# A hybrid decoder layer: the MLP's gate and up as seven block products, its down projection as a separate pass

## Chip, core, metric

One core of a Trainium2 chip runs the whole layer as one program. The metric is device time in microseconds; the kernel before takes 3286.72 us (median of 3 runs, 3285.8 to 3287.6). Engines: PE is TensorE (matrix products), PEld its weight loads, DVE is VectorE, ACT ScalarE, POOL GpSimd, and SP (SyncE) issues every DMA of this kernel.

## What is computed

A decoder layer on 2048 tokens of width 1024: token mixing (attention and a state space), cross-attention, and a gated MLP. Only the MLP changes:

```
hn   = rms_norm(h, norm_ffn)                       # [2048, 1024]
gate, up = split(hn @ w_ffn_up)                    # 2 x [2048, 2816]
gate = causal_dwconv(gate, conv_w, conv_b)         # 3 taps along the tokens
h    = h + (silu(gate) * up) @ w_ffn_down          # [2048, 1024]
```

All values are float32. A product a x b is done in three passes: each operand is split into a high part that TensorE's fp32r format holds exactly and a low remainder, and lo x hi, hi x lo and hi x hi are summed in PSUM (`mm3`, lines 63 to 67). A split is one ScalarE copy and one VectorE subtraction (`split`, lines 70 to 72).

## The kernel before

Everything is feature-major: 128 features on the partitions, tokens along the free axis, 512 tokens per PSUM bank. Order of the stages: input projection with the state space beside it, attention, `StageC` (output projection, cross-attention and its projection, 512 tokens at a time), then `StageD`, the MLP.

`StageC.run` ends with the cross-attention's output projection over four chunks c of 512 tokens. For each of 8 output tiles it does 24 products (8 feature tiles x 3 passes), loads h1 (L1390), adds (L1391) and stores the residual `h2D` (L1392). The operands of odd chunks lie in the pool `ca1`, those of even chunks in `even`, on the right side of SBUF. After chunk 2 the right side is handed on (`ahead`, `Dn.begin`), and the MLP's first loads run beside chunk 3.

`StageD.work` takes the tokens in two halves of 1024. Per half it holds the residual of 8 feature tiles in SBUF (`hacc`, L1413) and its scaled split (`hx`). The norm's factor r by token is applied behind the products. There are NFF = 22 tiles of 128 hidden features, in groups of four. Per tile: load and split the 512 KB weights of gate and up; for each 512 tokens 24 products for gate, the convolution, SiLU (VectorE, ScalarE, one GpSimd product, L1489 to L1499), 24 products for up, and the split of the result. After a group the down projection adds its share to `hacc` in SBUF: 8 output tiles x 2 token blocks, each of 12 products and one VectorE addition (L1511). So a half has 22 x 2 x 2 x 24 = 2112 products of gate and up and 1056 of down; both halves 4224 and 2112.

The code is written as a data flow. At build time a planner allocates the tiles and orders each engine's queue and SP's queue by the order of the text and by when it expects each input and buffer; the chip then runs each queue strictly in that order. A tile of a pool waits for the last reader of the buffer that it takes over.

Of the kernel before, what the change touches and what calls it, by code (L numbers as in the profile page):

```python
# [8 lines left out]
F32 = mybir.dt.float32  # L9
# [33 lines left out]
# columns of the packed [128, n] parameter array  # L43
# [55 lines left out]
def exp_acc(nc, scratch, out, x):  # L99
    """exp(x), x below 80, to float32's accuracy on VectorE (small tiles); scratch gives tiles of x's shape."""  # L100
# [15 lines left out]
class SumSq:  # L116
    """Sum over tiles of their squares, [128, n]."""
# [90 lines left out]
def stage_a(ctx, K, xT, win, wf, memT, wxk, wxv, qD, kD, vD, uD, cD, xkD, xvD, side):  # L208
    """Input projection.  First u^T (tokens step-major), then q^T and k^T (normalised, feature-major), f,
    and v as hi and lo; side(ctx) gives the steps of work that goes beside."""  # L210
# [24 lines left out]
    # the pools of the work beside lie below those of the first loads  # L235
# [4 lines left out]
    # with the tokens on partitions: 0.25 * eps * (mean square + eps) by heads, and -2 / rms  # L240
# [3 lines left out]
    # the forget gates' projection, [token in its tile, head, tile]  # L244
# [22 lines left out]
    # column tiles of 256 in win: q 0,1  k 2,3  v 4,5  u 6,7  # L267
# [39 lines left out]
    def qk_begin(p, j, w, g, dst):  # L307
        """256 columns of q or k of two token tiles, normalised by head."""
# [15 lines left out]
    def qk_end(f, p, j, g, dst):  # L324
        """Feature-major, with the norm's gain."""
# [39 lines left out]
def forget(K, tile_, pss, ft, cD):  # L365
    """Forget gate: cumsum(log_sigmoid(f + bias)), worked as [(head, block), token]."""
# [29 lines left out]
    # log f = min(z, 0) - log1p(e)  # L396
# [11 lines left out]
def s5_setup(ctx, K, uD):  # L408
    """Per-state constants of all groups, [(re, im) x state, group], in steps."""
# [4 lines left out]
    # kernels K_m for m = 7..-7 (zero below 0), [channel in, group, m, channel out]  # L414
# [6 lines left out]
    with tc.tile_pool(name="s5t", bufs=1, side="right", reuse_waits="tile") as sp:  # L421
# [36 lines left out]
        # powers lambda^0..8  # L458
# [20 lines left out]
        # decay over a step of 8, and the unit rotation  # L479
# [37 lines left out]
        # zero-order hold: B times (lambda - 1) / a  # L517
# [29 lines left out]
        # c1 = [c_re; -c_im], c2 = [-c_im; -c_re]  # L547
# [8 lines left out]
        # powers in the order of the steps: 7..0, and 8..1  # L556
# [6 lines left out]
        # D, to go into K_0  # L563
# [5 lines left out]
def s5_tables(K, S, sp, b, n=2):  # L569
    """Of groups nb..nb+n-1: the products' weights and the rotation tables."""  # L570
# [10 lines left out]
    def weights(r, i, mr, mi, name, tag):  # L581
        """r m_r + i m_i over (group, step, channel); r, i by step and group, m by group and channel."""
# [30 lines left out]
def s5_prep(K, S, pools, b, tables, n=2):  # L613
    """The products' weights as hi and lo, with the kernels of a chunk's own steps."""
# [14 lines left out]
    # row (step in i, channel in), column (step out 7 - o, channel out): K_{7 - o - i}  # L629
# [46 lines left out]
    # the state before each chunk  # L676
# [23 lines left out]
def s5(ctx, K, uD, yD):  # L700
    """The whole of it, in steps; ctx is the stack of pools around."""
# [21 lines left out]
class Head:  # L723
    """One head of the forgetting attention, in steps that another phase's steps can go between."""

    def __init__(self, K, h, P, qD, kD, vD, cD, oD, lD):
# [3 lines left out]
        # keys [k_hi; k_lo], cumsum on every partition, values [v_hi, v_lo] per key tile, row sums  # L730
# [6 lines left out]
    def prepare(self, fp=None):  # L737
        """Loads the keys, the values and the first queries."""
# [911 lines left out]
```

## Time and profile before

| | |
|---|---|
| median of 3 runs | 3286.72 us |
| profiled execution, first to last instruction (span) | 3283.0 us |
| around the span (median less span) | 3.7 us |
| MLP: first product to end of the span | 1794.3 to 3283.0 us |
| granted TensorE clock, mean over the span | 0.980 |

The profile is one execution. Its page gives the span and no total of its own, so the run's time is read as the span and the 3.7 us around it. Busy shares are averages over stages; what limits a stage is read from the windows and the waits of that stage. A clock of 1.00 is the higher of TensorE's two levels, 2.4 GHz.

### The profile page before, as it was taken

Reading aid. Unit: us, or ns where it says so; the run is one execution under the profiler, and the core shown is the slowest. Engines: PE = TensorE matmul, PEld = TensorE weight load, DVE = VectorE, ACT = ScalarE, POOL = GpSimd, SP = SyncE. Lnnn points to the kernel's source line nnn. Section 1 sums busy time; section 2 is a strip of 40 time slices with the busy share of each in tenths; the row PEclk is TensorE's granted clock in tenths of the full one; section 3 lists DMA queues with packets and bytes.
Section 4 is the critical chain, followed back from the end, with each engine's and each line's share of the span. In section 5 each row is a group of like instructions: output and inputs, shape, how many; then the busy total and the mean of one; then the engine's idle time right before and its main releaser. Section 6 shows DMA issues by size and latency. Waiting matters only on the chain.

```text
span 3283.0 us, 42856 instructions
## 1 busy us (share of the span) xinstructions
PE 3143.8 (96%) x16060; PEld 2617.5 (80%) x16060; DVE 1962.1 (60%) x3474; ACT 1236.4 (38%) x2256; POOL 522.9 (16%) x596
## 2 busy tenths in 40 slices
PE   7898878999999889999999999999999999999999
PEld 6788878888887667888787878888887788888887
DVE  8768899688878856444543544445445544445444
ACT  5443323488878524444422322212122312212121
POOL 3616664001001420000000100001000100001000
PEclk9898989999999999999999999999999999999999
DMA  6853434654444654212345211111113211111111
GB/s 192 159 181 116 143 112 127 189 150 133 116 147 130 183 164 159 76 54 76 120 138 170 61 45 52 45 45 52 45 47 130 68 52 52 39 52 48 43 45 61
DMA packets 253000, 329.50 MB, mean 100 GB/s; under 512 B 91636, under 2 KB 154356, under 8 KB 251640
## 3 DMA queue, kind: packets, MB, share of 16 engines
q1 hardware_dynamic: 252792, 326.76, 33.5%
q8 instruction: 126, 2.06, 0.3%
q14 instruction: 82, 0.67, 0.1%
HBM read 242.17 MB, written 84.52 MB: 100 GB/s over the span
## 4 chain that ended last, share of the span: by engine, by line
PE 78%; DVE 10%; DMA 5%; issue 2%; ACT 2%; POOL 2%; SPq 0%; DVEq 0%; ACTq 0%; POOLq 0%
PE dmm L66 10%; PE dmm L65 10%; PE dmm L67 10%; PE dps L66 5%; PE dps L65 5%; PE dps L67 5%; PE cmm L65 4%; PE cmm L66 4%; PE cmm L67 4%; PE pt L824 3%; PE po L817 2%; PE sps L790 2%; PE po L818 2%; PE sps L791 2%; DVE whl L72 1%
## 5 line engine op out<-in xcount | busy, mean ns | idle before, releaser
L65 PE MATMUL dmm<-hx,whl 128*128 128x512 f32 x1408 | 555.3, 395 | 2.1 <-ACT hx L77 2.1
L66 PE MATMUL dmm<-hx,whl 128*128 128x512 f32 x1408 | 555.5, 395 | 0.6 <-DVE hx L78 0.6
L67 PE MATMUL dmm<-hx,whl 128*128 128x512 f32 x1408 | 555.3, 395 | 0.0
L71 ACT CAST whl<-wraw 128x1024 fp32r<-128x1024 f32 (+3 forms) x251 | 218.0, 871 | 683.2 <-PE dps L67 402.5
L1499 POOL TENSOR_TENSOR gt<-gt,r 128x512 f32<-128x512 f32 x88 | 115.9, 1317 | 1886.3 <-DVE gt L1498 1282.7
L65 PEld LDWEIGHTS dmm<-hx,whl 128*128 128x128 f32 x1408 | 263.6, 187 | 68.4 <-ACT hx L77 3.0
L66 PEld LDWEIGHTS dmm<-hx,whl 128*128 128x128 f32 x1408 | 263.8, 187 | 66.5 <-DVE hx L78 1.2
L67 PEld LDWEIGHTS dmm<-hx,whl 128*128 128x128 f32 x1408 | 263.9, 187 | 65.0
L65 PE MATMUL cmm<-act,whl 128*128 128x512 f32 x760 | 307.2, 404 | 2.6 <-DVE whl L72 1.3
L66 PE MATMUL cmm<-act,whl 128*128 128x512 f32 x760 | 301.7, 397 | 4.1 <-DVE act L72 4.0
L1511 DVE TENSOR_TENSOR hacc<-dps,hacc 128x512 f32<-128x512 f32 x192 | 132.7, 691 | 281.6 <-PE dps L67 281.5
L67 PE MATMUL cmm<-act,whl 128*128 128x512 f32 x760 | 300.6, 396 | 0.0
L72 DVE TENSOR_TENSOR whl<-wraw,whl 128x1024 fp32r<-128x1024 f32 (+3 forms) x251 | 256.5, 1023 | 41.9 <-ACT whl L71 41.7
L66 PE MATMUL dps<-gl,whl 128*128 128x512 f32 x704 | 277.7, 394 | 0.6 <-DVE gl L72 0.6
L65 PE MATMUL dps<-gh,whl 128*128 128x512 f32 x704 | 277.8, 395 | 0.4 <-ACT gh L71 0.3
L67 PE MATMUL dps<-gh,whl 128*128 128x512 f32 x704 | 277.6, 394 | 0.0
L1489 DVE TENSOR_TENSOR g<-dmm,r 128x512 f32<-128x512 f32 x88 | 60.9, 692 | 240.8 <-PE dmm L67 240.8
L814 DVE TENSOR_TENSOR pl<-pt,ph 128x512 fp32r<-128x512 f32 (+1 forms) x320 | 186.8, 605 | 22.5 <-ACT ph L828 21.0
L824 PE MATMUL pt<-pk,sb 128*128 128x128 f32 x1088 | 173.7, 277 | 4.4 <-DVE pl L814 2.4
L66 PEld LDWEIGHTS cmm<-act,whl 128*128 128x128 f32 x760 | 144.3, 190 | 40.3 <-DVE act L72 6.7
L65 PEld LDWEIGHTS cmm<-act,whl 128*128 128x128 f32 x760 | 144.2, 190 | 38.9 <-issue 2.2
L828 ACT CAST ph<-pt 128x512 fp32r<-128x512 f32 (+1 forms) x320 | 158.8, 521 | 39.0 <-PE pt L824 36.6
(448 smaller groups left out, 6684.7 us busy)
## 6 DMA issues: line engine op xcount, KB each, us to landing
wraw<-wup SPq DMA_DIRECT2D x87, 512.0 KB
wraw<-wdn SPq DMA_DIRECT2D x80, 256.0 KB
qhl<-qD SPq DMA_DIRECT2D x128, 128.0 KB
wraw<-win SPq DMA_DIRECT2D x28, 512.0 KB
x<-xT SPq DMA_DIRECT2D x32, 256.0 KB
xr<-xT SPq DMA_DIRECT2D x32, 256.0 KB
kD<-qy SPq DMA_DIRECT2D x32, 256.0 KB
qD<-qy SPq DMA_DIRECT2D x32, 256.0 KB
```

The lines of the kernel that those rows point to most:

```text
L65: nc.tensor.matmul(out, lhsT=al, rhs=bh, start=first, stop=False)
L66: nc.tensor.matmul(out, lhsT=ah, rhs=bl, start=False, stop=False)
L67: nc.tensor.matmul(out, lhsT=ah, rhs=bh, start=False, stop=last)
L71: nc.scalar.copy(hi, src)
L72: (eng or nc.vector).tensor_tensor(lo, src, hi.bitcast(F32), op=ALU.subtract)
L790: nc.tensor.matmul(out, lhsT=ql[:, o : o + 128], rhs=kc, start=True, stop=False)
L791: nc.tensor.matmul(out, lhsT=qh[:, o : o + 128], rhs=kc, start=False, stop=not diag)
L814: v.tensor_tensor(b, c, a.bitcast(F32), op=ALU.subtract)
L824: nc.tensor.transpose(ps[:, j * 128 : (j + 1) * 128], rows[j][:, kt * 128 : (kt + 1) * 128], K.ident)
L828: nc.scalar.copy(ph[:, s], ps[:, s])
L1499: nc.gpsimd.tensor_tensor(t, t, r[:, s], op=ALU.mult)
L1511: v.tensor_tensor(acc[m][:, s], ps, acc[m][:, s], op=ALU.add)
```

## The change

Gate and up weights of one hidden tile form a 2 x 2 block matrix: rows gate and up, columns the two halves of the 1024 features (four 128-tiles each). The operand is 2 x 2 as well: feature halves by two token blocks of 512. The block product takes seven block multiplications in place of eight, with sums of blocks formed beforehand and afterwards. One block multiplication is 4 feature tiles x 3 passes = 12 products of 128 x 512, so one hidden tile and half has 7 x 12 = 84 products in place of 96. Step u runs over 2 x 22 = 44 of them.

- `StageD.sums` scales the residual with the gain and with r, forms the operand's sums on GpSimd and stores seven operands of four tiles to DRAM (`xsD`). The first half's runs beside chunk 3 of `StageC` (`side`), the second half's from u = 4.
- `StageD.operand` loads them back and splits them: 28 tiles per half, all held in `dx`.
- `fast_weights` forms four sums of weight blocks on GpSimd and splits seven blocks of 128 x 512 per step.
- After the products, sums are formed from PSUM: p6 and p7 add onto p1's bank once ScalarE has copied it (`kept`), p3 onto p5's.
- The activations go to DRAM (`hD`). `StageD.down` is a second pass over four blocks of 512 tokens: 8 output tiles, each 22 x 3 = 66 products into one PSUM bank, one addition of the reloaded residual, one store. Its weights are loaded once per token block, 32 x 1.4 MB.

The other lines of the diff delete comments. Its core:

```diff
+STEPS = ("p1", "p2", "p5", "p6", "p3", "p4", "p7")
+def fast_weights(K, pools, ra, rb, q):
+    wp, sp = pools
+    a11, a12, a21, a22 = ra[:, :q], ra[:, q:], rb[:, :q], rb[:, q:]
+    def s(x, y, op):
+        t = sp.tile([128, q, 128], F32, tag="ws", name="wsum")
+        gp.tensor_tensor(t, x, y, op=op)
+        return t
+    def hl(x):
+        t = wp.tile([128, 2, q, 128], F32R, tag="w", name="wf")
+        split(nc, t[:, 0], t[:, 1], x)
+        return t
+    s1 = s(a21, a22, ALU.add)
+    yield hl(a11)
+    s2 = s(s1, a11, ALU.subtract)
+    yield hl(a12)
+    yield hl(s1)
+    s4 = s(a12, s2, ALU.subtract)
+    yield hl(s2)
+    s3 = s(a11, a21, ALU.subtract)
+    yield hl(s4)
+    yield hl(a22)
+    yield hl(s3)
...
+    def begin(self, wup):
+        self.ap, self.rp, self.xp, self.sp = pool("da", 1), pool("dr", 4), pool("dxs", 6), pool("dws", 3)
+        self.acc = self.ap.tile([128, 512], F32, name="sums")
+        self.raws(0)
+        return self.sums(0)
...
+    def sums(self, half):
+        W = 256
+        for o in range(0, 512, W):
+            cols = slice(o, o + W)
+            new = lambda n: self.xp.tile([128, 2, W], F32, tag="xs", name=n)
+            r = new("xr")
+            nc.sync.dma_start(r, e(self.rD[half])[:, :, cols].broadcast_to([128, 2, W]))
+            for k in range(4):
+                s0, s1 = new("xs0"), new("xs1")
+                for t, i in ((s0, k), (s1, k + 4)):
+                    nc.sync.dma_start(t, e(self.h2D[half][i * 128 : (i + 1) * 128])[:, :, cols])
+                    v.scalar_tensor_tensor(out=t, in0=t, scalar=K.g_ffn[:, i : i + 1], in1=r, op0=ALU.mult, op1=ALU.mult)
+                n, t4 = new("xs2"), new("xs3")
+                gp.tensor_tensor(n[:, 1], s1[:, 1], s0[:, 1], op=ALU.subtract)
+                gp.tensor_tensor(s0[:, 1], s0[:, 1], s0[:, 0], op=ALU.subtract)
+                gp.tensor_tensor(n[:, 0], s1[:, 1], s0[:, 1], op=ALU.subtract)
+                gp.tensor_tensor(t4[:, 0], n[:, 0], s1[:, 0], op=ALU.subtract)
+                for t, ix in ((s0[:, 0], 0), (s0[:, 1], 2), (s1[:, 0], 1), (s1[:, 1], 4), (n[:, 0], 3), (n[:, 1], 6), (t4[:, 0], 5)):
+                    nc.sync.dma_start(self.xsD[half][ix, k][:, cols], t)
+                yield
+    def operand(self, half, dx):
+        for ix in range(7):
+            out = []
+            for k in range(4):
+                t = self.xp.tile([128, 512], F32, tag="xs", name="xb")
+                nc.sync.dma_start(t, self.xsD[half][ix, k])
+                x = dx.tile([128, 2, 512], F32R, tag="x", name="xf")
+                split(nc, x[:, 0], x[:, 1], t)
+                out.append(x)
+            yield out
...
+    def up(self, ctx):
+        dx, wp, gp, cp, tp, kp = pool("dx", 28), pool("dw", 8), pool("dg", 2), pool("dc", 4), pool("dt", 2), pool("dk", 1)
+        psm = pool("dpm", 2, space=PSUM)
...
+        for u in range(2 * NFF):
+            self.raws(u + 1)
...
+            if u == 4:
+                more = self.sums(1)
+            bank = {n: psm.tile([128, 512], F32, tag=n, name="d" + n) for n in "abed"}
...
+            for i, n in enumerate(STEPS):
+                last = u == NFF - 1
+                if i + 1 < 7:
+                    w[STEPS[i + 1]] = next(nw)
+                    if xs is not None:
+                        x[STEPS[i + 1]] = next(xs)
+                else:
+                    nw = later
+                    xs = self.operand(1, dx) if last else None
...
+                b = {"p1": "a", "p2": "b", "p5": "e", "p6": "a", "p3": "e", "p4": "d", "p7": "a"}[n]
+                product(bank[b], w[n], x[n], n in ("p1", "p2", "p5", "p4"))
+                if n == "p1":
+                    v.tensor_copy(g[:, 0:2], carry[:, f])
+                    p1 = kept(bank["a"], "kp1")
+                elif n == "p2":
+                    v.tensor_tensor(g[:, 2:514], bank["b"], p1, op=ALU.add)
+                    gate(0)
+                elif n == "p5":
+                    p5 = kept(bank["e"], "kp5")
+                elif n == "p6":
+                    u2 = kept(bank["a"], "ku2")
+                elif n == "p3":
+                    v.tensor_tensor(g[:, 514:], bank["e"], u2, op=ALU.add)
+                    v.tensor_copy(carry[:, f], g[:, 1024:])
+                    gate(1)
+                elif n == "p7":
+                    u3 = kept(bank["a"], "ku3")
+                    v.tensor_tensor(p5, bank["a"], p5, op=ALU.add)
+                    v.tensor_tensor(u3, u3, bank["d"], op=ALU.subtract)
+                    out(0, u3)          # GpSimd product, store to hD
+                    out(1, p5)
+                next(more, None)
...
+    def down(self, ctx, wdn, outT):
+        hp, wp, rp, op = pool("eh", 29), pool("ew", 2), pool("er", 3), pool("eo", 3)
+        psm = pool("epm", 4, space=PSUM)
+        def weights(i):
+            return load_w(K, wp, wdn[i % KT], [128, NFF, 128], parts=2)
+        def operand(c):
+            for k in range(NFF):
+                t = rp.tile([128, 512], F32, tag="hr", name="hraw")
+                nc.sync.dma_start(t, hD[c][k * 128 : (k + 1) * 128])
+                x = hp.tile([128, 2, 512], F32R, tag="h", name="hf")
+                split(nc, x[:, 0], x[:, 1], t)
+                yield x
+        w = weights(0)
+        nxt = list(operand(0))
+        for c in range(NC):
+            h, nxt = nxt, []
+            more = operand(c + 1) if c + 1 < NC else iter(())
+            for m in range(KT):
+                nw = weights(i + 1) if i + 1 < NC * KT else None
+                ps = psm.tile([128, 512], F32, tag="mm", name="dps")
+                nc.sync.dma_start(res, h2D[c // 2][m * 128 : (m + 1) * 128, c % 2 * 512 : c % 2 * 512 + 512])
+                for k in range(NFF):
+                    mm3(nc, ps, w[0][:, k], w[1][:, k], h[k][:, 0], h[k][:, 1], k == 0, k == NFF - 1)
+                    if m == KT - 1:
+                        nxt.extend([t for t in [next(more, None)] if t is not None])
+                v.tensor_tensor(res, ps, res, op=ALU.add)
+                nc.sync.dma_start(outT[m * 128 : (m + 1) * 128, cols], res)
+                w = nw
```

The function `gate` of the new loop keeps the convolution and SiLU of before (ScalarE identity, two VectorE passes, ScalarE tanh, one VectorE pass) on each of the two token blocks.

## Rows read from the trace of the kernel before

**Rows 1.** page, busy time: us, share of the span, instructions

```profile
PE 3143.8 (96%) x16060; PEld 2617.5 (80%) x16060; DVE 1962.1 (60%) x3474; ACT 1236.4 (38%) x2256; POOL 522.9 (16%) x596
```

**Rows 2.** page, costliest groups: products of gate and up, of down

```profile
L65 PE MATMUL dmm<-hx,whl 128*128 128x512 f32 x1408 | 555.3, 395 | 2.1 <-ACT hx L77 2.1
L65 PE MATMUL dps<-gh,whl 128*128 128x512 f32 x704 | 277.8, 395 | 0.4 <-ACT gh L71 0.3
```

**Rows 3.** windows: us, busy us of PE, PEld, DVE, ACT, POOL, clock, DMA, GB/s

```profile
1748.00:1766.00 18.00, 18.00 (x79) 14.50 (x79) 5.32 (x8) 3.16 (x5) 0.00 (x0) 1.00 0.86 300
1795.00:1815.00 20.00, 19.61 (x77) 15.67 (x78) 17.08 (x28) 15.28 (x23) 0.00 (x0) 0.91 0.51 157
2515.00:2555.00 40.00, 39.10 (x165) 30.34 (x164) 28.35 (x46) 15.77 (x26) 0.59 (x1) 1.00 0.78 266
2600.00:3278.00 678.00, 677.92 (x2906) 542.91 (x2905) 309.51 (x488) 143.90 (x199) 50.47 (x39) 1.00 0.16 48
```

**Rows 4.** timeline of TensorE, firsts and lasts of 87 and 85 products

```profile
1719.76 0.39 PE L66 MATMUL cmm<-act,whl 128*128 128x512 f32 x1
1739.87 0.40 PE L65 MATMUL cmm<-act,whl 128*128 128x512 f32 x1
1772.77 0.39 PE L67 MATMUL cmm<-act,whl 128*128 128x512 f32 x1
1791.81 0.39 PE L67 MATMUL cmm<-act,whl 128*128 128x512 f32 x1
```

**Rows 5.** groups by line and shape, 1800 to 3283 us: busy us, mean ns

```profile
L72 DVE TENSOR_TENSOR whl<-wraw,whl 128x512 fp32r<-128x512 f32 x80 | 55.4, 692 | 0.0
L1494 DVE SCALAR_TENSOR_TENSOR gt<-g,pk,gt 128x512 f32<-128x512 f32 x88 | 65.9, 749 | 23.0 <-ACT gt L1493 23.0
L1489 DVE TENSOR_TENSOR g<-dmm,r 128x512 f32<-128x512 f32 x88 | 60.9, 692 | 240.8 <-PE dmm L67 240.8
L71 ACT CAST gh<-gt 128x512 fp32r<-128x512 f32 x88 | 54.7, 621 | 161.7 <-DVE gt L1501 161.7
L1493 ACT ACTIVATE gt<-g,pk 128x512 f32<-128x512 f32 x88 | 71.7, 814 | 187.8 <-DVE g L1489 183.5 <-DVE carry L1491 4.4
L1497 ACT ACTIVATE th<-gt 128x512 f32<-128x512 f32 x88 | 55.6, 632 | 152.6 <-DVE gt L1495 152.6
L1499 POOL TENSOR_TENSOR gt<-gt,r 128x512 f32<-128x512 f32 x88 | 115.9, 1317 | 1886.3 <-DVE gt L1498 1282.7 <-DVE carry L1491 603.6
```

**Rows 6.** groups by line and shape, the whole span, same columns

```profile
L72 POOL TENSOR_TENSOR gl<-g,gh 128x256 fp32r<-128x256 f32 x32 | 23.6, 736 | 164.9 <-ACT gh L71 155.7 <-DVE pl L814 9.2
L1320 ACT COPY xoy<-xov 128x512 f32<-128x512 f32 x32 | 17.5, 592 | 3.6 <-PE xov L67 3.5
L72 DVE TENSOR_TENSOR whl<-wraw,whl 128x1024 fp32r<-128x1024 f32 x151 | 187.5, 1243 | 41.9 <-ACT whl L71 41.7
```

**Rows 7.** timeline of VectorE and GpSimd, 1207 to 1210 us

```profile
1207.34 1.44 POOL L1109 TENSOR_TENSOR fo<-fo 128x512 f32<-128x512 f32 x1 [5.89 <-DMA fo<-oD]
1207.58 1.75 DVE L72 TENSOR_TENSOR act<-nout,act 128x512 fp32r<-128x512 f32 x1
1208.86 1.61 POOL L1110 TENSOR_TENSOR fo<-fo,li 128x512 f32<-128x512 f32 x1
```

**Rows 8.** timeline of SyncE's DMA issues and of one ScalarE wait for a load

```profile
1749.85 3.02 SPq L1413 DMA_DIRECT2D hacc<-h2D  x5
1771.23 0.32 SPq L1392 DMA_DIRECT2D h2D<-h  x1
1773.24 0.32 SPq L1390 DMA_DIRECT2D h<-h1D  x1
1618.48 0.32 SPq L1195 DMA_DIRECT2D hl<-xoD  x1
1621.33 0.62 ACT L71 CAST act<-hl 128x512 fp32r<-128x512 f32 x1 [1.15 <-DMA hl<-xoD]
```

**Rows 9.** timeline of TensorE where the MLP begins

```profile
1794.31 0.49 PE L65 MATMUL dmm<-hx,whl 128*128 128x512 f32 x1 [2.12 <-ACT hx L77]
```

More of the change, by code (lines that the diff above doesn't have):

```diff
@@ L1380, in run @@
         nxt = hn
+        side = iter(())
         for c in range(NC):
@@ L1396, in run @@
                     end3(*late)
+                next(side, None)
             late = (c, sq.acc)
             if c + 2 == NC:
-                ahead()
+                side = ahead()
         self.ctx.close()
-class StageD:
-    def __init__(self, K, h2D, rD, right):
-        self.K, self.h2D, self.rD, self.right = K, h2D, rD, right
-    def load(self, half):
-        self.ac = [self.bp.tile([128, T // 2], F32, tag=f"ac{k}", name="hacc") for k in range(KT)]
-        for k in range(KT):
-            self.K.nc.sync.dma_start(self.ac[k], self.h2D[half][k * 128 : (k + 1) * 128])
-    def begin(self, wup):
-        self.bp = self.right.enter_context(self.K.tc.tile_pool(name="da", bufs=1, side="right", reuse_waits="tile"))
-        self.load(0)
-        self.acc = self.bp.tile([128, 512], F32, name="sums")
-        self.raw = self.bp.tile([128, KT, 128], F32, tag="r", name="graw")
-        self.K.nc.sync.dma_start(self.raw, wup[0])
+STEPS = ("p1", "p2", "p5", "p6", "p3", "p4", "p7")
@@ new lines, in up @@
+        pool = lambda n, b, **k: ctx.enter_context(tc.tile_pool(name=n, bufs=b, reuse_waits="tile", **k))
+        dx, wp, gp, cp, tp, kp = pool("dx", 28), pool("dw", 8), pool("dg", 2), pool("dc", 4), pool("dt", 2), pool("dk", 1)
+        psm = pool("dpm", 2, space=PSUM)
+        cw = kp.tile([128, 3, NFF], F32, name="cw")
+        cb = kp.tile([128, NFF], F32, name="cb")
+        v.tensor_scalar(out=cw, in0=K.p("convw").rearrange("p (i f) -> p i f", i=3), scalar1=0.5, scalar2=None, op0=ALU.mult)
@@ new lines, in up, with product, kept @@
+        v.tensor_scalar(out=cb, in0=K.p("convb"), scalar1=0.5, scalar2=None, op0=ALU.mult)
+        carry = kp.tile([128, NFF, 2], F32, name="carry")
+        v.memset(carry, 0.0)
+        def product(ps, w, x, first):
+            for k in range(4):
+                for j, (a, b) in enumerate(((1, 0), (0, 1), (0, 0))):
+                    nc.tensor.matmul(ps, lhsT=w[:, a, k], rhs=x[k][:, b], start=first and k + j == 0, stop=k == 3 and j == 2, skip_group_check=not first)
+        def kept(ps, n):
+            t = cp.tile([128, 512], F32, tag="c", name=n)
+            nc.scalar.copy(t, ps)
+            return t
@@ new lines, in up, with gate, out @@
+        wps = (wp, self.sp)
+        x, nx = {}, None
+        nw = fast_weights(K, wps, *self.raw.pop(0), 4)
+        xs = self.operand(0, dx)
+        w = {}
+        w[STEPS[0]] = next(nw)
+        x[STEPS[0]] = next(xs)
+        more = iter(())
+        for u in range(2 * NFF):
+            half, f = divmod(u, NFF)
+            self.raws(u + 1)
+            later = fast_weights(K, wps, *self.raw.pop(u + 1), 4) if u + 1 < 2 * NFF else iter(())
+            if u == 2:
+                st = psm.tile([128, 512], F32, tag="d", name="fst")
+                nc.tensor.matmul(st, lhsT=K.ones, rhs=self.acc, start=True, stop=True)
+                K.ln_exp()
+                rl = rinv(K, tp, st, 512, 1.0 / D, EPS, tag="t")
+                nc.sync.dma_start(self.rD[1][:, 512:], rl[0:1])
+            if u == 4:
+                more = self.sums(1)
+            bank = {n: psm.tile([128, 512], F32, tag=n, name="d" + n) for n in "abed"}
+            g = gp.tile([128, 2 + 1024], F32, tag="g", name="g")
+            hs = []
+            def gate(n):
+                o = 512 * n
+                a = lambda i: g[:, o + i : o + i + 512]
+                t = tp.tile([128, 512], F32, tag="t", name="gt")
+                nc.scalar.activation(t, a(2), AF.Identity, bias=cb[:, f : f + 1], scale=cw[:, 2, f : f + 1])
+                v.scalar_tensor_tensor(out=t, in0=a(1), scalar=cw[:, 1, f : f + 1], in1=t, op0=ALU.mult, op1=ALU.add)
+                v.scalar_tensor_tensor(out=t, in0=a(0), scalar=cw[:, 0, f : f + 1], in1=t, op0=ALU.mult, op1=ALU.add)
+                th = tp.tile([128, 512], F32, tag="th", name="th", bufs=1)
+                nc.scalar.activation(th, t, AF.Tanh)
+                v.scalar_tensor_tensor(out=t, in0=th, scalar=1.0, in1=t, op0=ALU.add, op1=ALU.mult)
+                hs.append(t)
+            def out(n, up):
+                nc.gpsimd.tensor_tensor(hs[n], hs[n], up, op=ALU.mult)
+                nc.sync.dma_start(hD[2 * half + n][f * 128 : (f + 1) * 128], hs[n])
+            for i, n in enumerate(STEPS):
[7 more added lines that the diff above has]
+                    xs = self.operand(1, dx) if last else None
+                    if u + 1 < 2 * NFF:
+                        w[STEPS[0]] = next(nw)
+                        nxt = next(xs) if xs is not None else x[STEPS[0]]
+                b = {"p1": "a", "p2": "b", "p5": "e", "p6": "a", "p3": "e", "p4": "d", "p7": "a"}[n]
[21 more added lines that the diff above has]
+                next(more, None)
+            x[STEPS[0]] = nxt
```

119 lines of the change are left out of this document (36 added, 83 removed).

## The prediction, before the result was known

> **What bounds the kernel now.** I read the page's busy times first: TensorE is busy 96% of the span, VectorE 60%, GpSimd 16% [rows 1]. A mean over stages proves little, so I took the windows next: in the MLP TensorE is busy for 677.92 of 678 us at a granted clock of 1.00, and even where the halves meet for 39.1 of 40 [rows 3]. The MLP waits only at its start, 2.12 us for its first split operand [rows 9]. So from 1794 us on the time is the number of products times their spacing; every other engine and the DMAs lie beside it. The spacing is 678 us / 2906 = 0.2333 us [rows 3]; 4224 products of gate and up and 2112 of down (three lines each of x1408 and of x704) [rows 2] make 6336 x 0.2333 = 1478 us of the 1483 us.
>
> The spacing has a second value. In chunk 3 of the stage before, 84 intervals take 1791.81 - 1772.77 = 19.04 us, 0.2267 each; in chunk 2, 86 take 1739.87 - 1719.76 = 20.11, 0.2338 each [rows 4]. Weights, shapes and clock are the same; only the place of the moving operand differs (pool `ca1` against `even`).
>
> **The change, part by part.**
>
> *Fewer products.* 44 x 84 = 3696 in place of 4224; down keeps 2112. At 0.2333 us the 528 that go are worth 123.2 us.
>
> *Their spacing.* The trace can't show it for the new tiles. Its ends are 0.2267 and 0.2338 [rows 4], so between a gain of 5808 x 0.0066 = 38 us and a loss of 3. I take 0.2267. The new operands are tiles of [128, 2, 512] in the first pool opened on the left (`dx`, then `eh`), as those of `ca1` are behind one of whole 64 KB, while `hx`, `gh` and `gl` lie behind the odd 176 bytes of `carry`. The new code opens the pool of `carry` last. This is a correlation, not a mechanism that I can show. 5808 x 0.2267 = 1316.7, so both terms together are 1478.4 - 1316.7 = -161.7 us.
>
> *The loop's other engines, per step of 84 x 0.2267 = 19.04 us.* VectorE: 7 weight splits x 0.692, two gates of 2 x 0.749 + 0.69, four passes on PSUM x 0.692 [rows 5], and two short copies: 12.3 us. ScalarE: 7 x 0.621 + 2 x (0.814 + 0.632) [rows 5] + 4 PSUM copies x 0.592 [rows 6] = 9.6. GpSimd: 4 weight sums and 2 output products x 1.317 [rows 5] = 7.9. DMA: 1 MB in and 0.5 MB out, 80 GB/s, where 300 were moved in a window [rows 3]. None reaches 19. The new waits of TensorE are on PSUM copies, with one product block of 2.7 us (p3 on p5's copy) or two (p6, p7) between, for a copy of 0.6; what queues behind on TensorE is only the next block. Weight splits may run up to eight blocks (22 us) ahead, so they give slack. Bounds: 0 (all hidden; it can't gain, the spacing is counted already) to 1 us per step, 44. I take 6.
>
> VectorE and GpSimd do not run freely beside each other: a subtraction of 0.69 us took 1.75 when it met a GpSimd sum, and ended only after it [rows 7]. The Trainium skill (SBUF — State Buffer, section "SBUF: two separate sides") says that a VectorE instruction with two SBUF inputs and a GpSimd instruction exclude each other for a whole instruction; these rows agree. By it 9.2 us of VectorE's pass and GpSimd's 7.9 can't overlap, 17.1 of 19.04, and the loop would still hold; its worse reading is a rival below.
>
> *Entry, the largest cost.* Before, the residual's loads were issued at 1749.85, when chunk 2 left its place [rows 8], and needed no arithmetic before the split. Now the first half's sums run from there, in 8 rounds (2 column halves x 4 tiles) through six buffers, one of them held by r: a round's second load waits for a buffer of the round before. A store took 2.0 us (issue 1771.23, its buffer reused at 1773.24), a load at most 2.85 (1618.48 to 1621.33) [rows 8]. A round is about 2.3 us of load, 0.75 of VectorE [rows 5], four GpSimd sums of 128 x 256 at 0.736 [rows 6]: 6.0. The first ends at about 1759 (weights and three loads ahead of it), the eighth at 1801, its stores at 1803.5; then load 2.5 and split 0.62 + 0.69: the first product at about 1807, where it was 1794.3: +13. Queued behind the waits on SP are the residual's loads and stores of chunk 3; PSUM's three banks cover 16 us of that, so I add nothing. In step 0 VectorE splits 28 operand tiles, 19.4 us, beside 7.5 of its own passes (the weights' splits are done by then): 27 against 19, +8. After a pause of 2.12 us the clock was 0.91 over 20 us [rows 3]; a pause of 15 costs about 1 more. Entry +22. Bounds: +5 (sums done within chunk 3) to +45 (rounds of 8.5 us).
>
> *The second half.* From u = 4 its sums take 16 x 0.75 of VectorE and 32 x 0.736 = 23.6 of GpSimd over some 50 us; the 22 us of splits ahead take that up: +2 (0 to 10). Where the halves meet 28 splits come again, but may start as each block of step 21 is done: in about 33 us VectorE has 33 / 19.04 x 12.3 + 19.4 = 40.7 to do, less 5.5 of weight splits done ahead, 35 for 33, and GpSimd in its way: some 6, less the 0.9 lost there before: +5 (0 to 15).
>
> *Up to down.* By the pools' sizes, a layout that I estimate, the first weight buffer of `down` takes over the tiles of the last activations. So the weights wait for ScalarE's copy 0.6, VectorE 0.7, two GpSimd products 2.6, the store 2.0, then their own load of 0.7 MB, some 4, and a split of 1408 columns, 1.7 on VectorE by 1.243 for 1024 [rows 6] with ScalarE's ahead of it: 13 us in which TensorE stands. The 22 operand tiles are loaded and split meanwhile. +13. If the buffer is free earlier, only the split remains: +3; if the operands come late as well, +20.
>
> *Down.* Per output tile 66 x 0.2267 = 15.0 us for 1.4 MB of weights and 0.5 MB of residual and output, 130 GB/s. In the last tile of a token block 5.8 MB of operands come too; 22 splits x 0.692 = 15.2 us of VectorE and 7.2 MB at 300 GB/s = 24 us, against 30 in which the next block needs its last tile. +1 at each of three: 3 (0 to 12). The old additions of `hacc` and splits of `gh`, `gl` go; they were hidden.
>
> The sum: -161.7 + 6 + 22 + 2 + 5 + 13 + 3 = -110.7. The profiled span 3283.0 becomes 3172.3; with the 3.7 us that lie around it (median 3286.7 less 3283.0), 3176.
>
> **Rivals.**
>
> *A, the spacing stays at 0.2333.* For it: all of the MLP of before ran so. Against: rows of the tile shape now used. 38.5 us dearer: 3214.
>
> *B, VectorE bounds the loop.* If every GpSimd instruction holds it for its whole length, as 1.75 for 0.69 suggests [rows 7], a step is 12.3 + 7.9 = 20.2 us, 1.2 over TensorE's: 44 x 1.2 = 51, 3227. Against: four of VectorE's passes per step read PSUM on one side, and GpSimd's part can fall into VectorE's waits.
>
> *C, slower: the in-order queue on VectorE.* Added to B, VectorE stands at the head of its queue for the gate's ScalarE results, as it did for 23.0 us over 88 passes at L1494 [rows 5] with much idle time around. If the planner can't fill these waits, with copies, sums and stores feeding back through few buffers, a step takes 22.6 us (2.4 over B), 3.56 over TensorE's: +157, 3333. It decides the sign from 110.7 / 44 = 2.5 us per step, that is 21.6. Against: the planner kept TensorE at 677.92 of 678 us with VectorE busy 309.51 [rows 3], and the splits lie eight blocks ahead.
>
> *D, nearly all is hidden:* entry +5, the rest +10: 3140. For it: the halves met at a cost of 0.9 us with 16 splits to do [rows 3].
>
> **From cases to numbers.** Likeliest, spacing 0.2267 and the costs above: 0.42, its own range 3150 to 3205. A 0.22, B 0.13, C 0.10, D 0.10, something about even 0.03. A measurement of this kernel can tell 0.2%, 6.6 us, from no change. Faster: 0.42 + 0.22 + 0.13 + 0.10 = 0.87, less 0.01 for B gone worse, 0.86; same 0.03; slower 0.11. The range 3140 to 3262 holds the likeliest, A, B and most of D; it leaves out C and the lowest of D.
>
> **What would show it.** In the loop: 84 products per step, intervals of 0.2267 (A: 0.2333), TensorE without waits and GpSimd at 40%. At entry: `xs` loads waiting on stores, the first product near 1807, step 0 of some 27 us waiting for VectorE's splits of `xf`. Between up and down: one gap of about 13 us, ended by the split of `whl` behind a load that waited for `hD`. In `down`: waits only at m = 0. I am wrong if steps of the loop wait on VectorE throughout, or if the entry takes more than 45 us.

## The result, and the profile after

The changed kernel takes 3228.9 us (median of 4 runs, 3224.1 to 3242.8) where the kernel before took 3286.3 beside it: 0.9835 of it, 95% interval 0.9813 to 0.9856. That is 57 us less; 110 were forecast. The profiled execution took 3229.7 us, its span is 3227.9.

The page's busy times, us and share of the span, to be read beside [rows 1]: TensorE has lost three points of busy share and 528 products.

```profile
PE 2999.8 (93%) x15532; PEld 2529.5 (78%) x15532; DVE 2173.5 (67%) x3472; ACT 1455.2 (45%) x2644; POOL 856.9 (27%) x836
```

The windows (columns as in [rows 3]) show where TensorE loses time:

```profile
1780.00:1820.00 40.00, 4.11 (x19) 3.06 (x17) 19.22 (x23) 6.23 (x11) 16.88 (x18) 0.60 0.63 200
1820.00:1860.00 40.00, 25.34 (x94) 19.30 (x94) 29.58 (x40) 24.02 (x41) 11.69 (x10) 0.76 0.77 252
1860.00:1900.00 40.00, 39.21 (x169) 31.76 (x170) 36.11 (x47) 21.00 (x34) 17.80 (x13) 1.00 0.31 99
1900.00:1940.00 40.00, 30.26 (x124) 23.88 (x122) 24.00 (x34) 11.58 (x21) 26.26 (x21) 0.94 0.47 153
1940.00:1980.00 40.00, 28.12 (x109) 22.31 (x110) 26.77 (x31) 12.47 (x22) 25.29 (x20) 0.85 0.58 180
1980.00:2020.00 40.00, 35.76 (x148) 28.99 (x147) 33.65 (x42) 16.31 (x28) 26.29 (x19) 0.91 0.55 187
2020.00:2060.00 40.00, 40.00 (x178) 33.14 (x177) 31.88 (x40) 19.17 (x32) 18.35 (x13) 1.00 0.24 80
2280.00:2320.00 40.00, 34.47 (x138) 27.29 (x137) 35.91 (x56) 25.43 (x47) 15.97 (x7) 0.91 0.64 210
2320.00:2360.00 40.00, 39.73 (x176) 32.57 (x175) 35.69 (x45) 19.27 (x34) 22.86 (x15) 1.00 0.30 95
2680.00:2720.00 40.00, 40.00 (x178) 33.14 (x177) 23.83 (x35) 15.88 (x26) 9.39 (x7) 1.00 0.13 46
2720.00:2760.00 40.00, 22.33 (x88) 16.78 (x87) 20.70 (x25) 15.68 (x22) 2.93 (x2) 0.83 0.63 218
2760.00:2800.00 40.00, 39.68 (x173) 31.84 (x173) 20.29 (x23) 15.90 (x19) 0.00 (x0) 1.00 0.77 242
```

2020 to 2060 is the loop undisturbed: TensorE without a pause. The start of a step repeats every 19.04 us / 84 products = 0.2267 us. The windows around it hold the losses. What TensorE waited for from 1780 us on, the first five lines of the view of waits (us in total, times, longest; a copy `kp` is ScalarE's copy out of PSUM):

```profile
PE da L1534 <- ACT xf L71: 48.8, 1, 48.8
PE de L1534 <- ACT kp L1538: 27.4, 7, 8.8
PE dps L65 <- DVE whl L72: 14.2, 1, 14.2
PE da L1534 <- ACT kp L1538: 4.5, 3, 3.1
PE dps L65 <- ACT hf L71: 3.8, 4, 1.8
```

The balance, each loss being the stretch less its products x 0.2267, so that waits and the slow clock behind them (0.60 to 0.94) are both in it (a product on the edge of two windows counts in both, which is some tenths of a us each):
- entry, from the last product of the stage before (1784.1) to 1900: 115.9 - 263 x 0.2267 = 56.3
- second half's sums, 1900 to 2020: 120 - 381 x 0.2267 = 33.6
- halves meeting, 2280 to 2360: 80 - 314 x 0.2267 = 8.8
- up to down, 2680 to 2800: 120 - 439 x 0.2267 = 20.5

That is 119.2, less about 5 that the kernel before lost at such places: 2.1 of wait and 2 of clock at its entry, 0.9 where its halves met [rows 3, 9]. With -161.7 for products and spacing, and -8.1 because the stage before, the same code, ended at 1784.1 in place of 1792.2 in this execution (1782 to 1796 over the runs below), the sum is -55.6; the spans differ by 55.1.

At the entry, SyncE's queue and VectorE's scalings of the sums (timeline: start, us):

```profile
1771.10 5.56 SPq L1493 DMA_DIRECT2D xsD<-xs  x7
1776.70 2.43 SPq L1484 DMA_DIRECT2D xs<-h2D  x2
...
1781.85 5.07 SPq L1493 DMA_DIRECT2D xsD<-xs  x7
...
1747.54 3.48 DVE L1485 SCALAR_TENSOR_TENSOR xs<-xs,sg_ffn,xr 128x512 f32<-128x512 f32 x2 [0.81 <-DMA xs<-h2D]
...
1822.54 2.41 DVE L1485 SCALAR_TENSOR_TENSOR xs<-xs,sg_ffn,xr 128x512 f32<-128x512 f32 x2
```

Seven stores hold SyncE for some 5 us while VectorE scales and GpSimd makes the sums one by one (from 1740 to 1830 us it stands ahead of such stores 22.0 us for VectorE and 16.1 for GpSimd), and the next round's loads stand behind them. The scalings of the first and the eighth round start 75 us apart, 10.7 a round.

### The profile page after: what moved, and what is told of

Its sections match the earlier page's. It is cut to its first block, busy times and chain, and to the rows that moved or that the text cites. A ratio compares the mean times of both kernels' runs of the same rounds, so it can differ in the third digit from the quotient of the medians.

```text
span 3227.9 us, 43874 instructions
## 1 busy us (share of the span) xinstructions
PE 2999.8 (93%) x15532; PEld 2529.5 (78%) x15532; DVE 2173.5 (67%) x3472; ACT 1455.2 (45%) x2644; POOL 856.9 (27%) x836
## 4 chain that ended last, share of the span: by engine, by line
PE 66%; DVE 12%; DMA 8%; POOL 4%; issue 4%; ACT 3%; SPq 1%; POOLq 0%; DVEq 0%; ACTq 0%
PE da L1534 9%; PE de L1534 6%; PE dps L66 4%; PE dps L65 4%; PE dps L67 4%; PE cmm L65 4%; PE cmm L66 4%; PE cmm L67 4%; PE pt L824 3%; PE dd L1534 3%; PE db L1534 3%; PE sps L790 2%; PE po L817 2%; PE po L818 2%; PE sps L791 2%
## 5 line engine op out<-in xcount | busy, mean ns | idle before, releaser
L1534 PE MATMUL da<-xf,wf 128*128 128x512 f32 x1584 | 380.4, 393 | 55.0 <-ACT xf L71 48.8
L1534 PEld LDWEIGHTS da<-xf,wf 128*128 128x128 f32 x1584 | 299.2, 189 | 120.5 <-ACT xf L71 49.4
L71 ACT CAST whl<-wraw 128x1024 fp32r<-128x1024 f32 (+2 forms) x132 | 156.1, 1206 | 317.2 <-PE dps L67 241.6
L65 PE MATMUL dps<-hf,whl 128*128 128x512 f32 x704 | 274.9, 391 | 18.0 <-DVE whl L72 14.2
L1534 PE MATMUL de<-xf,wf 128*128 128x512 f32 x1056 | 264.1, 399 | 28.1 <-ACT kp L1538 27.4
L66 PE MATMUL dps<-hf,whl 128*128 128x512 f32 x704 | 274.7, 391 | 0.2 <-DVE hf L72 0.2
L67 PE MATMUL dps<-hf,whl 128*128 128x512 f32 x704 | 274.3, 390 | 0.0
L1534 PEld LDWEIGHTS de<-xf,wf 128*128 128x128 f32 x1056 | 203.2, 193 | 74.9 <-ACT kp L1538 30.6
L72 DVE TENSOR_TENSOR whl<-wraw,whl 128x1024 fp32r<-128x1024 f32 (+2 forms) x132 | 189.7, 1454 | 56.4 <-ACT whl L71 55.2
L65 PEld LDWEIGHTS cmm<-act,whl 128*128 128x128 f32 x760 | 144.9, 191 | 40.8 <-issue 6.1
L66 PEld LDWEIGHTS cmm<-act,whl 128*128 128x128 f32 x760 | 145.1, 191 | 40.2 <-DVE act L72 6.6
L828 ACT CAST ph<-pt 128x512 fp32r<-128x512 f32 (+1 forms) x320 | 159.0, 521 | 37.8 <-PE pt L824 35.4
L72 DVE TENSOR_TENSOR wf<-wraw,wf 128x512 fp32r<-128x512 f32 x132 | 158.1, 1202 | 20.0 <-ACT wf L71 19.9
L67 PEld LDWEIGHTS cmm<-act,whl 128*128 128x128 f32 x760 | 144.6, 190 | 32.9
L65 PEld LDWEIGHTS dps<-hf,whl 128*128 128x128 f32 x704 | 132.5, 188 | 47.8 <-DVE whl L72 14.7
```

The source lines that it names most:

```text
L71: nc.scalar.copy(hi, src)
L72: (eng or nc.vector).tensor_tensor(lo, src, hi.bitcast(F32), op=ALU.subtract)
L828: nc.scalar.copy(ph[:, s], ps[:, s])
L1534: nc.tensor.matmul(ps, lhsT=w[:, a, k], rhs=x[k][:, b], start=first and k + j == 0, stop=k == 3 and j == 2, skip_group_check=not first)
```

## The experiments

Ratios are to the kernel before, run beside each on the same chip; the changed kernel's is 0.9835. One hundredth is 33 us.

**Where the spacing comes from: e1, e2, e9, e10.** e1 is the kernel before with one tile elsewhere:

```
+lp = pool("dl", 1)          # opened last
-carry = hp.tile([128, NFF, 2], F32, name="carry")
+carry = lp.tile([128, NFF, 2], F32, name="carry")
```

> The kernel before, with the 176 bytes of `carry` in a pool opened last, so that hx, gh and gl start on multiples of 128 bytes (addresses mod 128: 64 before, 0 now); nothing else is changed and no product is taken away. Theory (where the moving operand starts sets the spacing): dmm and dps products come every 0.2267 us in place of 0.2333, 6336 x 0.0066 = 42 us less, about 3244 us. Rival (the shorter spacing of the changed kernel belongs to its shorter runs of products or its separate passes): spacing stays 0.2333, 3286 us.

3243.2 us, 0.9874 (0.9858 to 0.9891): 41 us from moving 176 bytes. The windows have 2649 products in 600 us, 0.2265 each, for 2906 in 678 [rows 3]:

```profile
2600.00:3200.00 600.00, 600.00 (x2649) 1.00 0.16 46
```

So most of what the changed kernel gained is not the change's: against e1, by the two ratios, it is 0.4% faster, 13 us, and the two intervals almost touch.

e2 shifts the changed kernel's operands:

```
+ctx.enter_context(tc.tile_pool(name="shu", bufs=1)).tile([128, 16], F32, name="shu")
 dx, wp, ... = pool("dx", 28), pool("dw", 8), ...      # the same ahead of "eh"
```

> The changed kernel with 64 bytes opened ahead of the pools of the moving operands in both passes (xf and hf start at 64 mod 128 in place of 0). Theory (placement): spacing 0.2333, 5808 x 0.0066 = 38 us more, about 3267 us, less what the slower products hide of the waits (a few us). Rival (something else in the changed kernel made the spacing): 3229 us, spacing 0.2267.

A miss: 3229.4 us, 0.9837, spacing unchanged (its windows below). The operand's own start isn't it. But the 64 bytes shift the weights' pool behind it too. In e9 and e10 the tile ahead of the operands and one between operands and weights differ:

```
+pool("su1", 1).tile([128, 16], F32, name="su1")   # e9: 64 B;  e10: 192 B
 dx = pool("dx", 28)
+pool("su2", 1).tile([128, 48], F32, name="su2")   # e9: 192 B; e10: none
 wp, ... = pool("dw", 8), ...
 # down: e9 64 B between "eh" and "ew"; e10 192 B ahead of "eh", 64 B between
```

> The changed kernel; gate and up: operands at 64 mod 256 bytes, weights at 0; down: operands at 0, weights at 64 (both were at 0, and both at 64 in the run with a shift of 64, whose spacing stayed at 0.2267 us). Theory (what counts is where moving operand and weights lie to each other): 0.2333 us in both passes, about 38 us more. Rival (the moving operand's own start counts, with 64 harmless and the 192 of the kernel before harmful): 0.2267 us in both passes, 3229 us.

> The changed kernel; gate and up: operands and weights both at 192 mod 256 bytes; down: operands at 192, weights at 0, as the kernel before had them. Theory (relative place): 0.2267 us in gate and up, 0.2333 us in down, 14 us more. Rival (the operand's own start): 0.2333 us in both, 38 us more. If down keeps 0.2267 us, the place is not it at all.

e9 took 3256.7 us, e10 3247.8 (one run each). Windows of gate and up, then of down, clock, DMA share and GB/s behind the count of products; first e2:

```profile
2400.00:2660.00 260.00, 260.00 (x1149) 1.00 0.26 84
2800.00:3180.00 380.00, 380.00 (x1678) 1.00 0.51 169
```

The same two windows of e9, where both are slower:

```profile
2400.00:2660.00 260.00, 260.00 (x1138) 1.00 0.26 82
2800.00:3180.00 380.00, 380.00 (x1631) 1.00 0.51 170
```

And of e10, where only down is:

```profile
2400.00:2660.00 260.00, 260.00 (x1149) 1.00 0.25 84
2800.00:3180.00 380.00, 380.00 (x1631) 1.00 0.50 166
```

The places are worked out from the sizes and the order of the pools; no profile shows an address. Of (operand, weights) modulo 256 bytes: (0, 0), (64, 64) and (192, 192) run at 0.2267; (192, 0) and (0, 64) at 0.2333, as the kernel before had it with (192, 0). What counts is where the two lie to each other: operand less weights is 0 modulo 256 in the three fast cases and 192 in both slow ones. (64, 0), a difference of 64, gives a third value, neither theory's: e9's steps in gate and up start 19.23 us apart, 0.2289, a third of the way as if one product in three were slow:

```profile
2501.95 2.91 PE L1537 MATMUL dd<-xf,wf 128*128 128x512 f32 x12
...
2521.18 2.91 PE L1537 MATMUL dd<-xf,wf 128*128 128x512 f32 x12
```

It was tried in gate and up alone. Why a third, and by what mechanism at all, stays open.

**The entry: e16, e4, e5, e6.** e16 leaves the first half's sums out:

```
-return self.sums(0)
+return iter(())
-nc.sync.dma_start(t, self.xsD[half][ix, k])
+nc.sync.dma_start(t, self.xsD[1][ix, k] if half else self.h2D[0][k * 128 : (k + 1) * 128, :512])
```

> The changed kernel without the first half's sums (its operands are read from the residual itself, so the first half's output is not the reference's). If the sums are the whole of the entry's cost but for the splits: the first product 5 to 8 us after the last of the stage before, step 0 of some 27 us, together 33 to 40 us less, 3189 to 3196 us. If the splits of the operand and the clock after the pause carry more of it: 3200 to 3215 us.

3188.1 us, 0.9708 (0.9689 to 0.9728): by the ratios 42 us of the entry's 56 are the sums; the rest holds the wait for the first product, now 5.6 us, the 28 splits and the clock:

```profile
1794.81 5.36 PE L1534 MATMUL da<-xf,wf 128*128 128x512 f32 x12 [5.59 <-DVE wf L72]
```

e4, e5 and e6 ask what makes a round 10.7 us. e5 has the buffers of e4 alone; e6 the order alone, by another engine:

```
-pool("dxs", 6), ... pool("dw", 8)
+pool("dxs", 8), ... pool("dw", 7)                    # e4, e5
+nxt = load(k + 1)      # ahead of the stores of round k: e4
-nc.sync.dma_start(self.xsD[half][ix, k][:, cols], t)
+gp.dma_start(self.xsD[half][ix, k][:, cols], t)      # e6
```

> The changed kernel with the loads of the sums' next round ahead of the stores of the round before in SP's queue, and two more buffers for it (8, and 7 in place of 8 for the weights). Theory (SP's queue, in which a round's loads stand behind seven stores that wait for GpSimd, makes the rounds of 10 us): rounds of 6 to 7 us, the first product about 25 us earlier, a smaller dip in the second half's sums, together 25 to 45 us less, 3185 to 3205 us. Rival (GpSimd's sums, 0.8 to 1.1 us each with the other engines beside them, or VectorE at the head of its queue make them): rounds of 9 us or more, 3215 to 3230 us.

> The changed kernel with 8 buffers for the sums in place of 6 and 7 for the split weights in place of 8, SP's order left to be what follows from it: the buffers of the run with the loads ahead, without its order. If the order was what shortened the rounds: rounds of 10 us as in the changed kernel, 3225 to 3232 us. If it was the buffers: rounds near 7 us, 3203 to 3212 us.

> The changed kernel with the sums' stores issued by GpSimd in place of SP. Theory (SP's in-order queue is what makes the first half's rounds long and what holds hD's stores back in the second half's): rounds of 6 to 7 us and the waits of TensorE on copies after u = 4 down from 26 us to under 10, 3180 to 3195 us. Rival (GpSimd itself is the limit, and seven issues a round make it longer): rounds of 9 us or more, 3225 us or more.

e4: 3203.5 us, 0.9763 (0.9746 to 0.9779), rounds of 7.0:

```profile
1757.82 1.23 DVE L1493 SCALAR_TENSOR_TENSOR xs<-xs,sg_ffn,xr 128x512 f32<-128x512 f32 x1
...
1764.83 0.75 DVE L1493 SCALAR_TENSOR_TENSOR xs<-xs,sg_ffn,xr 128x512 f32<-128x512 f32 x1
...
1771.83 0.93 DVE L1493 SCALAR_TENSOR_TENSOR xs<-xs,sg_ffn,xr 128x512 f32<-128x512 f32 x1
```

One scaling of each of three rounds is shown. TensorE's wait falls from 48.8 to 24.1. e5: 3221.9 us, 0.9819 (0.9802 to 0.9835, which overlaps the changed kernel's), rounds of 10.1, wait 45.1. e6: 3231.6 us, 0.9842 (0.9827 to 0.9856), rounds of 10.3. So neither buffers nor order alone: with six buffers the loads wait for stores of the round before even when SyncE is free (in e6, from 1740 to 1830 us, six times, 16.7 us), and with eight they stand behind those stores in SyncE's queue. e6 is no clean test of the queue, for in it each store takes GpSimd some 0.56 us, about 4 us a round. The Trainium skill (DMA: Bandwidth & Descriptors, section "Issuing engines are not separate DMA queues") says that issuing from several engines saves only the issuing time; e6's 3231.6 us is in line with that.

**The second half's sums: e3, e8, e11, e14, e17.**

```
-more = self.sums(1)
+more = iter(())                                     # e3; operand from xsD[0]
-next(more, None)
+if i in (0, 4): next(more, None)                    # e8
-t = tp.tile([128, 512], F32, tag="t", name="gt")
+t = tp.tile(..., name="gt", bufs=4)                 # e11, e17; "dw" 7
-v.scalar_tensor_tensor(out=t, in0=t, scalar=K.g_ffn[...], in1=r, ...)
+gp.tensor_tensor(t, t, r, op=ALU.mult)              # e14, e17; second half
```

> The changed kernel without the second half's sums (its operand is read from the first half's store, so the second half's output is not the reference's). Theory (the waits of TensorE on copies between u = 4 and u = 9 come from these sums: late loads at the head of VectorE's and SP's queues): TensorE busy without waits from 1900 to 2020, 30 to 35 us less, about 3196 us. Rival (the splits of weights ahead run out there, or the clock after the entry is to blame): the waits stay, 3225 us or more.

> The changed kernel with the second half's sums asked for in two blocks of a step (8 rounds over 4 steps of 19 us) in place of every block. Theory (they cost 33 us because they come faster than GpSimd, the loads and the stores can follow, and the gates stand behind them in in-order queues): the waits of TensorE on copies from u = 4 on fall from 26 us to under 8, 20 to 30 us less, 3200 to 3209 us. Rival (each round costs TensorE its time however they are spread, a load at the head of VectorE's queue being late each time): the same waits over a longer stretch, 3222 us or more.

> The changed kernel with four buffers for the gates' tile t in place of two (and 7 for the split weights in place of 8). Theory (in the second half's sums ScalarE stands at the next step's gate until hD's stores of this step's two tiles, queued behind the sums on GpSimd and SP, give t back, and the copy that TensorE waits for stands behind it): the waits on copies fall from 26 us to under 8, 20 to 28 us less, 3200 to 3209 us. Rival (VectorE at the head of its queue, waiting for a load, holds the gate and through it ScalarE, whatever buffers t has): 3222 us or more.

> The changed kernel with the second half's scaling on GpSimd in place of VectorE, so that no instruction of the second half's sums stands in VectorE's queue (its gain g_ffn is left out there, so the second half's output is not the reference's). Theory (VectorE's wait at the head of its queue is what reaches TensorE): waits on copies fall from 26 us to under 10, 15 to 25 us less, 3204 to 3214 us; what may remain is GpSimd's out products and weight sums behind its own waits. Rival (GpSimd is the engine that is late): the waits grow, 3230 us or more.

> The changed kernel with both edits that did nothing alone: the second half's scaling on GpSimd (its gain left out there, so its output is not the reference's) and four gate buffers (7 for the split weights). Theory (two waits in series, VectorE's for loads and ScalarE's for hD's stores, each hidden behind the other): the waits on copies after u = 4 fall from 26 us to under 12, 15 to 25 us less, 3204 to 3214 us. Rival (GpSimd is late in its work itself, weight sums included): 3225 us or more, with TensorE waiting for weights or copies as before.

e3: 3201.3 us, 0.9753 (0.9731 to 0.9774), 27 us by the ratios; the spans of the profiled executions are 34.5 apart, and TensorE is busy for all of 1900 to 2020: the 33.6 us are these sums. The four others missed: e8 3231.4 us (0.9852), e11 3228.6 (0.9834), e14 3239.2 (0.9854), e17 3229.3 (0.9849). TensorE's waits on ScalarE's copies, 1780 to 2100: 26.0 us in the changed kernel (23.2 to 26.8 in e2, e7, e9 and e10, which leave these sums as they are), 25.1 in e8, 21.4 in e11, 33.4 in e14, 24.0 in e17. They hardly fell; the traces show them moving. What did lower them is e5's eight buffers for the sums, to 17.2; with the loads ahead as well (e4) they are 17.5, no less (one execution each).

In the changed kernel's first long wait the gate's product stands behind the sums in GpSimd's queue, though VectorE had its inputs done at 1904.9. hD's stores go out as soon as the products end, the gate's buffer comes free late, and ScalarE stands:

```profile
1908.78 0.72 POOL L1490 TENSOR_TENSOR xs<-xs,xs 128x256 f32<-128x256 f32 x1
...
1909.46 1.26 POOL L1579 TENSOR_TENSOR gt<-gt,kp 128x512 f32<-128x512 f32 x1
...
1910.74 1.54 SPq L1580 DMA_DIRECT2D hD<-gt  x2
...
1912.84 0.81 ACT L1570 ACTIVATE gt<-g,cb,cw 128x512 f32<-128x512 f32 x1 [7.85 <-DMA hD<-gt]
```

In its longest one VectorE stands for a load, the gate's addition behind it, and ScalarE waits for that:

```profile
1969.15 0.75 DVE L1485 SCALAR_TENSOR_TENSOR xs<-xs,sg_ffn,xr 128x512 f32<-128x512 f32 x1 [4.08 <-DMA xs<-h2D]
...
1971.60 0.81 ACT L1570 ACTIVATE gt<-g,cb,cw 128x512 f32<-128x512 f32 x1 [9.52 <-DVE g L1601]
...
1972.93 4.35 PE L1534 MATMUL de<-xf,wf 128*128 128x512 f32 x12 [8.83 <-ACT kp L1538]
```

With four gate buffers (e11) VectorE stands for a load too; the gate's addition, whose product ended near 1930.6, comes at 1938.5, then ScalarE's gate, then the copy, then TensorE:

```profile
1932.84 0.75 DVE L1485 SCALAR_TENSOR_TENSOR xs<-xs,sg_ffn,xr 128x512 f32<-128x512 f32 x1 [2.97 <-DMA xs<-h2D]
...
1938.50 0.68 DVE L1601 TENSOR_TENSOR g<-db,kp 128x512 f32<-128x512 f32 x1
...
1939.21 0.81 ACT L1570 ACTIVATE gt<-g,cb,cw 128x512 f32<-128x512 f32 x1 [7.92 <-DVE g L1601]
...
1940.55 4.45 PE L1534 MATMUL de<-xf,wf 128*128 128x512 f32 x12 [4.47 <-ACT kp L1538]
```

With no sums on VectorE and four gate buffers (e17) GpSimd stands for the load, its product of the gate behind it, and ScalarE waits for that buffer:

```profile
1974.42 1.26 POOL L1486 TENSOR_TENSOR xs<-xs,xr 128x512 f32<-128x512 f32 x1 [3.70 <-DMA xs<-h2D]
...
1975.64 1.26 POOL L1582 TENSOR_TENSOR gt<-gt,kp 128x512 f32<-128x512 f32 x1
...
1976.93 0.59 ACT L1541 COPY ku<-da 128x512 f32<-128x512 f32 x1 [9.11 <-POOL gt L1582]
...
1977.57 7.88 PE L1537 MATMUL da<-xf,wf 128*128 128x512 f32 x24 [8.09 <-ACT ku L1541]
```

My theories of one wait, and of two in series, fell. In three of the four places an in-order queue reaches the use of a load before it has landed (3.0 to 4.1 us, behind which ScalarE waits 7.9 to 9.5); in the first the load was 0.8 us late, and GpSimd's own work ahead of the gate's product made the wait. How the 26 us divide between late loads and the work in the queues stays open.

**Up to down: e7.**

```
-hp, wp, rp, op = pool("eh", 29), pool("ew", 2), pool("er", 3), pool("eo", 3)
+wr, rp = right("ewr", 2), right("er", 12)      # over the sums' tiles
+wp, hp, op = pool("ew", 2), pool("eh", 29), pool("eo", 3)
```

> The changed kernel with the pools of the pass down laid elsewhere: its raw weights and 12 raw operand buffers (in place of 3) over the tiles of the sums, which are free long before, its split weights over the operand tiles of the first products of the last step. Theory (between up and down TensorE stands because `down`'s first weights and operands take over tiles that the last activations hold): the gap of 14 us shrinks to 2 or 3 us and the late operands behind it go, 15 to 20 us less, 3210 to 3214 us. Rival (SP's queue, which stands at the last stores of hD, holds the loads back whatever their tiles): the gap stays above 10 us, 3225 us or more.

3219.2 us, 0.9818 (0.9800 to 0.9837): about 6 by the ratios, less than expected and with intervals that overlap. In the trace the first gap of 14.2 became two (2680 to 2800: 486 products, 9.8 us lost for 20.5):

```profile
2722.20 0.76 PE L65 MATMUL dps<-hf,whl 128*128 128x512 f32 x1 [4.38 <-DVE whl L72]
...
2725.32 0.79 PE L66 MATMUL dps<-hf,whl 128*128 128x512 f32 x1 [2.35 <-DVE hf L72]
```

**Together: e12, e13, e15, e18.** e12 has the edits of e4, e7 and e11 (6 buffers for the weights); e13 adds that of e8. e15 and e18 replace the round:

```
+rw = self.ap.tile([128, 2, 512], F32, tag="r", name="xr")     # r whole
+for t, a, b in ((s0, 0, 2), (s1, 1, 4), (n, 3, 6)):           # pairs: 4 stores for 7
+    nc.sync.dma_start(self.xsD[half][a : b + 1 : b - a, k][:, :, cols].rearrange("i p t -> p i t"), t)
+nxt = load(*rounds[j + 1])       # e18: ahead across the column halves too
```

> The loads ahead, the four gate buffers (weights' buffers 6) and the pools of down laid elsewhere, together. If they add up: 25 us of the loads ahead, 10 of the pools and what is left of the second half's waits, 10 to 17: 3177 to 3190 us. If the gates' buffers do nothing: 3192 to 3197 us. If six weight buffers are too few beside the sums: above 3200 us.

> The kernel with the loads ahead, gate buffers and pools of down (3186 us) with the second half's rounds asked for in two blocks of a step, so that a round's loads are issued some 9 us before VectorE needs them. Theory (VectorE stands at the head of its queue for a late load, the gate's addition behind it, then ScalarE's copy, then TensorE; spacing did nothing alone because the loads were still issued just ahead of their use): waits on copies between 1870 and 2000 fall from 19 us to under 6, 12 to 18 us less, 3168 to 3175 us. Rival (GpSimd's and VectorE's work beside the loop's is too much wherever it stands): 3182 us or more.

> The changed kernel with the loads ahead, r loaded whole once for each half, the sums stored in pairs (4 stores a round in place of 7), spaced rounds in the second half, and the pools of down laid elsewhere. From the 3186 us of the run with three of these: r whole takes away the 12 us between the two column halves less one round, -5; four stores in place of seven take 3 x 0.53 us of SP's time from a round of 6.9, to about 5.5 if SP is what limits it, 8 rounds, -10; spacing -12: 3155 to 3165 us. If GpSimd's four sums limit the round, only r and spacing: 3168 to 3175 us.

> The changed kernel with each round's loads ahead of the round before's stores, across the column halves too, r whole, paired stores, spaced rounds, three gate buffers, and the pools of down laid elsewhere. Against the run without the last load ahead and with two gate buffers (3185 us): entry 3 to 5 us shorter, waits on copies after u = 4 from 18 us to 5 to 10: 3170 to 3178 us. If GpSimd's rounds beside the loop are the limit: 3180 us or more.

e12 3186.1 us, 0.9705 (0.9691 to 0.9720); e13 3185.7, 0.9695 (0.9677 to 0.9713); e15 3185.3, 0.9693 (0.9678 to 0.9707); e18 3178.8, 0.9691 (0.9677 to 0.9706). e12 takes off 43 us by the ratios, where e4, e7 and e11 alone took 24, 6 and nothing; the intervals allow that they simply add up. By the ratios the other three can't be told from it, so spacing the rounds, r whole and fewer stores brought no measurable time, against what was expected of e13, e15 and in part e18. The first three lines of e18's waits, from 1780 us on:

```profile
PE da L1542 <- ACT xf L71: 17.1, 1, 17.1
PE de L1542 <- ACT kp L1546: 17.1, 5, 5.5
PE dps L65 <- DVE whl L72: 4.4, 1, 4.4
```

It is 0.9691 of the kernel before where e1, the old algorithm with its tile moved, is 0.9874: the change, block products and separate pass together, is worth 1.8% once its entry, its sums and the step from up to down are mended.

## Why the prediction was wrong

- *Products and spacing, -161.7:* right. 44 x 84 products come every 0.2267 us, and down's at the same. The hint (placement) was right, but it is the operand's place to the weights', not the operand's own; e1 shows that the 38 us were to be had without the change.
- *Loop, +6 (0 to 44):* no loss. VectorE is busy 32 of 40 us, 15.2 a step where I summed 12.3; no wait comes of it. Rivals A, B and C are refuted by the window 2020 to 2060, D by the losses.
- *Entry, +22 (5 to 45):* this step failed. 56.3 were lost, 52 more than before, past the bound and past the prediction's own sign of being wrong (more than 45). The pause was mis-sized, 48.8 for 15, because "A round is ...: 6.0" measured 10.7. The chain was the one that I summed, load, scaling, sums, next load, but its terms were too small. The timelines of SyncE, VectorE and GpSimd give, as means of rounds two to eight: 4.0 us from a round's first load to its first scaling (I had 2.3), 2.0 for two scalings, the second load landing later (0.75), 3.7 for four sums (2.9), and 0.7 until SyncE is past the last store and comes to the next load (nothing). e4, in which the next load no longer waits for the stores, gives 7.0; e5 and e6, with half of that, 10. The eighth round's sums, set to end at 1801, ended at 1828.2. Behind the pause, splits and clock (0.60 and 0.76 in two windows) cost 7.5 us for the 9 that I allowed.
- *Second half's sums, +2 (0 to 10):* this step failed too; 33.6. "The 22 us of splits ahead take that up" looked at the wrong cover: TensorE had its weights and waited for copies out of PSUM, which have one block of 2.7 us of slack. The prediction named the in-order queues only as a rival over the whole loop, not for the four steps in which late loads and the sums stand in them.
- *Halves meeting, +5 (0 to 15):* 8.8, in its bounds; 5.8 of it are waits and the rest clock.
- *Up to down, +13 (3 to 20):* the gap was 14.2, ended by the split of `whl` as said; with the operands late as well (four waits, 3.8 us) and the clock at 0.83 it came to 20.5, just over the upper bound.
- *Down, +3:* nothing measurable.

Direction and range held, the range by luck: the total lies beside rivals A (3214) and B (3227), which the loop refutes, and comes from two losses that each went past its bound. In the spans the forecast was 55.6 us too low (3172.3 for 3227.9): +30 from the entry (52 for 22), +32 from the second sums (33.6 for 2), +10 from the two joints, -9 from loop and down that cost nothing, -8 from a stage before that ended early; together 55.

## What to carry to other kernels

Before a change is credited with a faster engine, read the addresses of what that engine reads: moving one small tile gave the old kernel 41 of the 57 us. Work that is hung beside a full loop is priced by the queues it stands in, not by its busy time: for each load ask what stands ahead of it at its issuer, and for each user of it what stands behind. If two or more queues share such a load, giving one of them slack mostly moves the wait. What helped here were more buffers for the shared tiles (e5, beside the loop), and at the entry buffers and earlier loads together (e4).

## What was not expected of the hardware

Spacing of products of 512 columns, weights changed at each one, clock 1.00: 0.2267 us where operand and weights start at the same place modulo 256 bytes (three such places), 0.2333 at (192, 0) and (0, 64), 0.2289 at (64, 0). And taking all the stores of the sums off SyncE brought nothing (3231.6 us); GpSimd, which issued them, was busy 37.8 of 40 us in one window of that run.
